# Block 1's rope, global and dilated attention in one section with a written order of PE, DVE and ACT

## The chip, the cores and the metric

The kernel runs on one core of one Trainium2 chip. The metric is the device time of one execution in microseconds. Five engines work side by side, each on its own list of instructions in order: TensorE (PE, matmuls and transposes), VectorE (DVE), ScalarE (ACT), GpSimd (POOL) and SyncE (SP, which issues most transfers).

## The reference

A network of two layers is run on 256 tokens of width 1024: first Block 1 of both layers, then Block 2 of both. The change touches the mixer of Block 1 only:

```python
proj = h @ w_in
qa, ka, va, qd, kd, vd, gates = split(proj)             # 512, 128, 128, 768, 768, 768, 2048
qa = apply_rope(rms_norm(qa, qn_g)); ka = apply_rope(rms_norm(ka, kn_g))
out_a = global_gqa(qa, ka, va)                          # 8 heads of 64, 2 k/v heads, softmax over 256 keys
out_b = dilated(qd, kd, vd)                             # 12 heads in 3 groups, distance bias, softmax over all 3 groups
g_a, g_b = split(sigmoid(gates))
merged = g_a * (out_a @ w_pa) + g_b * (out_b @ w_pb)
return merged @ w_o
```

Behind it stand a residual with layer norms, and a mixture of 16 experts with a router. Six vectors per layer (shifts, scales and gates) come from a matrix `ada` times the conditioning vector.

## The kernel before, in words

All weights are float32 and are streamed once. A block of 1 MB lands in one of four raw buffers (`wraw`, issued by SP in program order). ACT casts each half of it to a rounded float (`hi`, L60, tile `whi`), DVE subtracts to get the rest (`lo`, L66, tile `wlo`), and PE does three matmuls in place of one: data-high by weight-high, data-low by weight-high, data-high by weight-low (`mm3`, L251 to L253). A block of w_in is 48 such matmuls of 256 columns (blocks 9 and 10, the dilated v, 24 of 512).

Each `ada` piece is four more 1 MB blocks, summed on DVE: two scalar-times-matrix sums of 128x1024 a block (L465, L467), then a few tiny matmuls with ones (`ada_cols`, `ada_row`). The loads are spread as background work: `wblk` pops one (`tick`) after each weight block, and the attention parts pop some by the tables `TJ` and `TU`. The sums of a load come at the next tick (`settle`).

Block 1's mixer (L951) starts when q, k and v of the global attention stand in PSUM. 17 weight jobs remain: three blocks of dilated q, three of k, three of v (one PSUM bank each for two token halves in the first two), eight of gates. Between them: rope and RMS norm of q and k on DVE (the norm factor is multiplied into q, L1017, and k, L1021), transposes of q and k on PE (L1028, L1033) with copies on ACT; then four pairs of global heads: scores (L1044), maximum on DVE, exponential on ACT (L379), shares on DVE (L385), transposes on PE (L392), copies on ACT (L395), values (L404). Then four dilated steps (two head pairs by two token halves): scores (L1092), bias on DVE (L1097), exponentials, shares, transposes (L1116), copies (L1118), values. The jobs are closures in a list, and `fill` puts one between two attention parts. Within this program order a scheduler chooses the order of instructions on each engine from its own estimates, so a cast can move ahead of a copy that was written before it. PSUM has two banks for scores and small sums (`sb`), two for transposes (`tp`) and four for products (`acc`).

Behind the mixer come w_pa (2 blocks), w_pb (1), w_out (4), the router's weights and the experts (16).

Of the kernel before, what the change touches and what calls it, by code (L numbers as in the profile page):

```python
# [15 lines left out]
DEPTH = 2  # L16
# [156 lines left out]
class Net:  # L173
    def __init__(self, tc, a, out, ctx, dbg=None):
        self.tc, self.nc, self.a, self.out = tc, tc.nc, a, out
        self.dbg_hook = dbg
        self.ctx = ctx
        P = lambda name, bufs, **k: ctx.enter_context(tc.tile_pool(name=name, bufs=bufs, **k))
        self.const = P("const", 1)
        self.big = P("big", NB8)  # L180
        self.wr = P("wr", NRAW)
        self.wh = P("wh", NHL)
        self.wl = P("wl", NHL)
        self.bg = []
        self.fills = []
        self.pend = None
# [256 lines left out]
    def ada_piece(self, l, pc, fin, row=False):  # L443
# [15 lines left out]
        def add(k, r):  # L459
            acc = box["acc"]  # L460
            for i in range(2):
                f = 2 * k + i
                rv = r[:, i * D:(i + 1) * D]
                if f == 0 and not row:
                    nc.vector.tensor_scalar_mul(acc, rv, self.cond[:, 0:1])  # L465
                else:
                    nc.vector.scalar_tensor_tensor(acc, rv, self.cond[:, f:f + 1], acc, op0=OP.mult, op1=OP.add)  # L467
            if k == 3:
                fin(acc)

        def go(k):
            r = load(k)
            self.settle()
            self.pend = lambda: add(k, r)
        return [lambda k=k: go(k) for k in range(4)]

    def settle(self):

        if self.pend:
            self.pend()  # L480
            self.pend = None

    def ada_cols(self, l, acc, dst, f0, n, off, j, plus):

        nc = self.nc
        ps = self.sb()
# [7 lines left out]
    def ada_row(self, acc, scale):  # L494
# [3 lines left out]
        for h in range(2):  # L498
            ps = self.tp()
# [451 lines left out]
    def mixer(self, l, hT):  # L951
# [17 lines left out]
        gt = [self.b8([128, 8, 256], name="gate") for _ in range(2)]  # L969

        def fm_job(i, dst, func, scale, ps=None):
            hl = self.wblk(w[i], 8)
            ps = self.fm_bank(hT, hl, 0, 8, ps=ps and ps())
            nc.scalar.activation(dst, ps, func, scale=scale)

        def vd_job(dst, n, srcs):
            bk, = self.proj_tm(hT, [(srcs, n)])
            for t in range(2):
                nc.scalar.copy(dst[:, t], bk[t])
        for dst, i0, sc in ((qdT, 3, 0.125), (kdT, 6, 1.0)):  # L980
            for b in range(3):
                self.fills.append(lambda i=i0 + b, d=dst[:, 2 * b:2 * b + 2], sc=sc:
                                  fm_job(i, d, AF.Copy, sc, self.sb if i < 3 + NSB[l] else None))
        self.fills.append(lambda: vd_job(vd0, 512, [w[9], w[10]]))
        self.fills.append(lambda: vd_job(vd1, 256, [w[11]]))
# [4 lines left out]
        qrs = []  # L990
        krs = []
        for t in range(2):
            nc.scalar.copy(va[:, t], kva[t][:, 128:256])
            for which, src, nh in ((0, qa[t][:, :512], 8), (1, kva[t][:, :128], 2)):
                rs = self.head_rstd(src, nh)
                if which == 0:
                    v = self.small([128, 16], "rs8", 2)
                    nc.vector.tensor_scalar_mul(v[:, :nh], rs, 0.125)
                    rs = v[:, :nh]
                A = self.t2([128, nh, 64], name="ropeA")  # L1000
                B = self.t2([128, nh, 32, 2], name="ropeB")
                s3 = src.rearrange("p (h d) -> p h d", d=64)
                s4 = src.rearrange("p (h d e) -> p h d e", d=32, e=2)
                cc = rt[:, which, t, 0][:, None, :].to_broadcast([128, nh, 64])
                nc.vector.tensor_mul(A, s3, cc)
                sv = rt[:, which, t, 1].rearrange("p (d e) -> p d e", e=2)
                for e in range(2):
                    nc.vector.tensor_mul(B[:, :, :, e], s4[:, :, :, 1 - e],
                                         sv[:, None, :, e].to_broadcast([128, nh, 32]))
                nc.vector.tensor_add(A, A, B.rearrange("p h d e -> p h (d e)"))  # L1010
                o = self.t2([128, 512], name="roped")
                rb = rs[:, :, None].to_broadcast([128, nh, 64])
                if which == 0:

                    for s in range(2):
                        ov = o.rearrange("p (j s d) -> p j s d", j=4, s=2)[:, :, s]
                        nc.vector.tensor_mul(ov, A[:, s * 4:(s + 1) * 4],  # L1017
                                             rs[:, s * 4:(s + 1) * 4, None].to_broadcast([128, 4, 64]))
                    qrs.append(o)
                else:  # L1020
                    nc.vector.tensor_mul(o[:, :128].rearrange("p (h d) -> p h d", d=64), A, rb)  # L1021
                    krs.append(o)
        for jj in range(2):
# [7 lines left out]
        p = self.tp()  # L1031
        for t in range(2):
            nc.tensor.transpose(p[:, t * 128:(t + 1) * 128], krs[t][:, :128], self.ident)  # L1033
        nc.scalar.copy(kaT, p[:, :256])
        oa = self.b8([128, 2, 4, 256], R, name="oa")
        zz = self.small([128, 2, 8], "att_z", 2)

        def scores(j):
            pr = []
            for h in range(2):  # L1040
                s = self.sb()
                hs = slice(h * 64, (h + 1) * 64)
                for t in range(2):
                    nc.tensor.matmul(s[:, t * 256:(t + 1) * 256], qaT[hs, j, t * 128:(t + 1) * 128], kaT[hs, :],  # L1044
                                     start=True, stop=True)
                n = 2 * j + h
                pr.append(self.exps(s.rearrange("p (n w) -> p n w", n=2), [zz[:, t, n:n + 1] for t in range(2)]))
            return pr

        def values(j, pr):  # L1050
            rz = self.small([128, 2, 2], "att_rz", 2)
            nc.vector.reciprocal(rz, zz[:, :, 2 * j:2 * j + 2])
            pts = []
            for h in range(2):
                self.share(pr[h], rz[:, :, h])
                pts.append(self.p_fm(pr[h]))
            if j % 2 == 0:
                bank["o"] = self.acc("oacc")
            o = bank["o"][:, j % 2 * 256:(j % 2 + 1) * 256]
            self.two_heads(o, [[pt[:, c] for c in range(2)] for pt in pts],  # L1060
                           [[va[:, c, h * 64:(h + 1) * 64] for c in range(2)] for h in range(2)])
            self.split_to(oa[:, 0, j], oa[:, 1, j], o)
        bank = {}
        self.bg_on = True
        for j in range(4):
            pr = scores(j)
            if j == 1:
                nc.gpsimd.dma_start(d01, a["k_dist"][:, :, 0:2])
                nc.gpsimd.dma_start(d2, a["k_dist"][:, :, 2])
            if j in TJ[l]:  # L1070
                self.tick()
            self.fill()
            values(j, pr)
        if l == DEPTH - 1:
            self.decay_log(0)

        self.fill(len(self.fills))
        for i in range(2):
            for b in range(4):
                self.fills.append(lambda i=i, b=b: fm_job(12 + 4 * i + b, gt[i][:, 2 * b:2 * b + 2], AF.Tanh, 0.5))  # L1080
        ob = self.sm.tile([128, 2, 2, 256], R, name="ob", tag="s4b", bufs=2)
        zz = self.small([128, 2, 8], "att_z", 2)
        od = self.acc("obacc")
        for jp in range(2):
            for t in range(2):
                sb = [self.sm.tile([128, 3, 256], F, name="sbias", tag="z1", bufs=NZ1) for _ in range(2)]
                for gs in ((0, 1), (2,)):
                    ss = [self.sb() for _ in range(2)]
                    for g in gs:
                        for i in range(2):  # L1090
                            hs = slice(i * 64, (i + 1) * 64)
                            nc.tensor.matmul(ss[i][:, g % 2 * 256:(g % 2 + 1) * 256],  # L1092
                                             qdT[hs, 2 * g + jp, t * 128:(t + 1) * 128], kdT[hs, 2 * g + jp, :],
                                             start=True, stop=True)
                    for g in gs:
                        for i in range(2):
                            nc.vector.scalar_tensor_tensor(sb[i][:, g], dist[t][g], -SLOPES[4 * g + 2 * jp + i],  # L1097
                                                           ss[i][:, g % 2 * 256:(g % 2 + 1) * 256],
                                                           op0=OP.mult, op1=OP.add)
                rz = self.small([128, 2], "att_rz", 2)  # L1100
                pts = []
# [844 lines left out]
```

## Time and profile before

| | us |
|---|---|
| median of 3 runs (lowest, highest) | 1745.29 (1740.69, 1746.53) |
| the profiled execution | 1744.94 |
| its span, first to last instruction | 1743.1 |
| Block 1's section, layer 0 (56.30 to 236.60) | 180.3 |
| Block 1's section, layer 1 (492.40 to 668.50) | 176.1 |

The section is counted from the end of the qkv matmuls to the first matmul of w_out. The mean granted clock of PE over the span is 0.984 of full speed. In the tables of stretches the columns are the stretch, its length, then busy microseconds of each engine with the number of instructions in brackets, the granted clock of PE, the share of the DMA engines and GB/s.

### The profile page before, as it was taken

Reading aid. Unit: us, or ns where it says so; the run is one execution under the profiler, and the core shown is the slowest. Engines: PE = TensorE matmul, PEld = TensorE weight load, DVE = VectorE, ACT = ScalarE, POOL = GpSimd, SP = SyncE. Lnnn points to the kernel's source line nnn. Section 1 sums busy time; section 2 is a strip of 40 time slices with the busy share of each in tenths; the row PEclk is TensorE's granted clock in tenths of the full one; section 3 lists DMA queues with packets and bytes.
Section 4 is the critical chain, followed back from the end, with each engine's and each line's share of the span. In section 5 each row is a group of like instructions: output and inputs, shape, how many; then the busy total and the mean of one; then the engine's idle time right before and its main releaser. Section 6 shows DMA issues by size and latency. Waiting matters only on the chain. (4 is left out here: it accounts for less than half of the span.)

```text
span 1743.1 us, 26009 instructions
## 1 busy us (share of the span) xinstructions
PE 1667.9 (96%) x10498; PEld 1451.3 (83%) x10498; DVE 1219.7 (70%) x1657; ACT 890.6 (51%) x1272; POOL 155.0 (9%) x187
## 2 busy tenths in 40 slices
PE   7899998999989999899999999999999999999999
PEld 6788886777778898677778889899987888989997
DVE  7888788879888857887986575655546457565453
ACT  1555446667554445666755454444435345454442
POOL 2200022200120002110020300000001120000000
PEclk9899999999999999989999999999999999999999
DMA  8777662889677744388965534455555463545551
GB/s 317 289 272 274 236 250 89 317 311 341 224 251 265 274 161 140 122 318 316 352 240 196 175 134 170 172 181 192 173 194 218 139 216 121 171 152 187 186 180 70
DMA packets 56334, 374.09 MB, mean 215 GB/s; under 512 B 6896, under 2 KB 7056, under 8 KB 14224
## 3 DMA queue, kind: packets, MB, share of 16 engines
q1 hardware_dynamic: 50256, 352.41, 56.4%
q0 software_dynamic: 5952, 19.97, 3.5%
q8 instruction: 84, 1.38, 0.3%
q14 instruction: 42, 0.34, 0.1%
HBM read 370.25 MB, written 2.10 MB: 214 GB/s over the span
## 5 line engine op out<-in xcount | busy, mean ns | idle before, releaser
L66 DVE TENSOR_TENSOR wlo<-wraw,whi 128x1024 fp32r<-128x1024 f32 x562 | 675.6, 1222 | 308.2 <-ACT whi L60 303.7
L60 ACT CAST whi<-wraw 128x1024 fp32r<-128x1024 f32 x572 | 587.6, 1049 | 437.3 <-PE acc L252 207.2
L251 PE MATMUL acc<-fm_hi,whi 128*128 128x256 f32 x1536 | 440.0, 286 | 0.0
L252 PE MATMUL acc<-fm_lo,whi 128*128 128x256 f32 x1536 | 436.0, 284 | 0.0
L253 PE MATMUL acc<-fm_hi,wlo 128*128 128x256 f32 x1536 | 435.5, 284 | 0.0
L251 PEld LDWEIGHTS acc<-fm_hi,whi 128*128 128x128 f32 x1536 | 294.7, 192 | 10.0 <-issue 8.9
L252 PEld LDWEIGHTS acc<-fm_lo,whi 128*128 128x128 f32 x1536 | 295.1, 192 | 3.7 <-issue 3.7
L253 PEld LDWEIGHTS acc<-fm_hi,wlo 128*128 128x128 f32 x1536 | 294.9, 192 | 1.8 <-issue 1.8
L262 POOL TENSOR_TENSOR rs_r<-rs_v,mhalf 128x1 f32<-128x1 f32 (+3 forms) x52 | 58.6, 1128 | 973.0 <-DVE rs_v L261 965.8
L251 PE MATMUL acc<-whi,fm_hi 128*128 128x512 f32 (+1 forms) x384 | 137.6, 360 | 3.1 <-ACT fm_hi L323 3.1
L253 PE MATMUL acc<-whi,fm_lo 128*128 128x512 f32 (+1 forms) x384 | 135.7, 354 | 4.2 <-DVE fm_lo L324 4.1
L252 PE MATMUL acc<-wlo,fm_hi 128*128 128x512 f32 (+1 forms) x384 | 135.9, 354 | 1.3 <-DVE wlo L66 1.3
L251 PE MATMUL gu<-whi,hgh 128*128 128x512 f32 x256 | 106.2, 415 | 5.1 <-DVE dT L669 2.9
L252 PE MATMUL gu<-wlo,hgh 128*128 128x512 f32 x256 | 103.7, 405 | 1.5 <-DVE wlo L66 1.5
L253 PE MATMUL gu<-whi,hgl 128*128 128x512 f32 x256 | 102.7, 401 | 0.0
L467 DVE SCALAR_TENSOR_TENSOR ada_acc<-wraw,cond,ada_acc 128x1024 f32<-128x1024 f32 x74 | 94.5, 1277 | 0.8
L253 PEld LDWEIGHTS acc<-whi,fm_lo 128*128 128x128 f32 x384 | 74.5, 194 | 15.1 <-DVE fm_lo L324 5.7
L252 PEld LDWEIGHTS acc<-wlo,fm_hi 128*128 128x128 f32 x384 | 74.5, 194 | 13.6 <-DVE wlo L66 4.9
L251 PEld LDWEIGHTS acc<-whi,fm_hi 128*128 128x128 f32 x384 | 74.4, 195 | 13.3 <-ACT fm_hi L323 4.1
L251 PE MATMUL acc<-whi,act_hi 128*128 128x512 f32 x176 | 68.5, 389 | 0.0
L252 PE MATMUL acc<-wlo,act_hi 128*128 128x512 f32 x176 | 68.5, 389 | 0.0
L253 PE MATMUL acc<-whi,act_lo 128*128 128x512 f32 x176 | 68.5, 389 | 0.0
(386 smaller groups left out, 2612.1 us busy)
## 6 DMA issues: line engine op xcount, KB each, us to landing
wraw<-in_moe SPq DMA_DIRECT2D x96, 1024.0 KB, 5.4
wraw<-in_win SPq DMA_DIRECT2D x58, 1024.0 KB, 5.4
wraw<-in_ffi SPq DMA_DIRECT2D x44, 1024.0 KB, 4.8
wraw<-in_ada SPq DMA_DIRECT2D x40, 1024.0 KB, 5.0
wraw<-in_wg SPq DMA_DIRECT2D x32, 1024.0 KB, 4.9
wraw<-in_ffo SPq DMA_DIRECT2D x22, 1024.0 KB, 4.8
wraw<-in_wo SPq DMA_DIRECT2D x16, 1024.0 KB, 4.9
wraw<-in_ada SPq DMA_DIRECT2D x16, 512.0 KB, 7.9
```

The costliest lines, as they stand in the source:

```text
L60: net.nc.scalar.copy(h, self.r[:, i * 1024:(i + 1) * 1024])
L66: (eng or net.nc.vector).tensor_sub(l, self.r[:, i * 1024:(i + 1) * 1024], h.bitcast(F))
L251: mm(ps, l[0], r[0], start=first, stop=False)
L252: mm(ps, l[0], r[1], start=False, stop=False)
L253: mm(ps, l[1], r[0], start=False, stop=last)
L262: nc.gpsimd.tensor_tensor(r[:, :n], v[:, :n], self.mhalf[:, :n], op=OP.pow)
L467: nc.vector.scalar_tensor_tensor(acc, rv, self.cond[:, f:f + 1], acc, op0=OP.mult, op1=OP.add)
```

## The change

The rope, the global attention, the dilated attention and the 17 weight jobs become one section in which the order of PE, DVE and ACT is the order in which the code is written. POOL and SP are still placed by the scheduler. The section is built from small pieces (`hi`, `lo`, `mm`, `ev`, `S`, `X`, `N`, `T`, `V` and, for the dilated part, `DS`, `DX`, `DN`, `DT`, `DV`). Block n+1 is cast and split while block n is multiplied, in step n. From step 3 on, each step loads one `ada` block and does the two sums of the one before at two places (`t0`, `t1`); before, 24 blocks were loaded in layer 0's section, now 14, and the other ten go behind it. Their last tiny matmuls are put off to the next tick and use an `acc` bank. The q norm factor is no longer multiplied into q: it scales the scores inside the exponential (a second per-partition operand) and the maximum (a tiny DVE multiply). Shares of the second head of each pair and all dilated shares move from DVE to ACT, and copies of transposed shares go back into the same tile.

```diff
-        self.fill(2)                                   # first two jobs, rope and attention between fills
-        for j in range(4):
-            pr = scores(j)
...
-            if j in TJ[l]:
-                self.tick()
-            self.fill()
-            values(j, pr)
...
+        def X(j):
...
+                nc.vector.tensor_reduce(nm[:, :2], s3, axis=AX.X, op=OP.max, negate=True)
+                nc.vector.tensor_tensor(nm[:, :2], nm[:, :2], rsq[:, :, n], op=OP.mult)
+                p = self.t2([128, 2, 256], name="prob")
+                for t in range(2):
+                    nc.scalar.activation(p[:, t], s3[:, t], AF.Exp, bias=nm[:, t:t + 1], scale=rsq[:, t, n:n + 1],
+                                         accum_out=zz[:, t, n:n + 1])
...
+        self.defer = True
+        with self.tc.manual_schedule(engines={E.DVE, E.Activation, E.PE}):
...
+            for i in range(4):
+                mm(0, i)
+            ev(0)
+            load(2)
+            rope(0, 0)
+            hi(1, 0)
+            lo(1, 0)
+            for t in range(2):
+                k_norm(t)
+            rope(1, 0)
+            k_tr()
+            hi(1, 1)
+            lo(1, 1)
...
+            for i in range(2):
+                mm(1, i)
+            q_tr(0)
+            mm(1, 2)
+            q_tr(1)
+            mm(1, 3)
+            ev(1)
+            load(3)
+            hi(2, 0)
+            lo(2, 0)
+            hi(2, 1)
+            lo(2, 1)
+            S(0)
+            X(0)
+            for i in range(4):
+                mm(2, i)
+            ev(2)
+            hi(3, 0)
+            lo(3, 0)
+            N(0)
+            hi(3, 1)
+            lo(3, 1)
...
+            for j in range(4):
+                n = 3 + j
+                load(n + 1)
+                t0, t1 = self.tick2()
+                if j < 3:
+                    S(j + 1)
+                    hi(n + 1, 0)
+                    X(j + 1)
+                else:
+                    DS(0, (0, 1))
+                    hi(n + 1, 0)
+                T(j)
+                mm(n, 0)
+                lo(n + 1, 0)
+                do(t0)
+                hi(n + 1, 1)
+                V(j)
+                mm(n, 1)
...
+                lo(n + 1, 1)
+                do(t1)
+                for i in (2, 3):
+                    mm(n, i)
+                ev(n)
+            if l == DEPTH - 1:
+                self.decay_log(0)
...
+            for u in range(4):
+                n = 9 + 2 * u
+                load(n + 1)
+                t0, t1 = self.tick2()
+                if u < 3:
+                    DS(u + 1, (0, 1))
+                hi(n + 1, 0)
+                DT(u)
+                lo(n + 1, 0)
+                do(t0)
+                mm(n, 0)
+                mm(n, 1)
+                hi(n + 1, 1)
+                if u < 3:
+                    DS(u + 1, (2,))
+                DV(u)
+                lo(n + 1, 1)
...
+                ev(n)
+                n += 1
+                load(n + 1)
+                t0, t1 = self.tick2()
+                hi(n + 1, 0)
+                lo(n + 1, 0)
+                mm(n, 0)
+                mm(n, 1)
...
+                ev(n)
+            self.sums()
```

In the order of ACT at the opening of the section in layer 0, `dil<-sb` is the eviction of a dilated q job, `sq` a square for a norm, `kaT` the copy of the transposed k. Before:

```order
15 L60 CAST whi<-wraw 128x1024 x2
16 L279 ACTIVATE sq<-acc 128x512
17 L60 CAST whi<-wraw 128x1024 x2
18 L279 ACTIVATE sq<-acc 128x128
19 L974 ACTIVATE dil<-sb 128x512
20 L279 ACTIVATE sq<-acc 128x512
21 L60 CAST whi<-wraw 128x1024 x2
```

and after:

```order
11 L60 CAST whi<-wraw 128x1024 x4
12 L1210 COPY va<-acc 128x128 x2
13 L281 ACTIVATE sq<-acc 128x128 x2
14 L1026 ACTIVATE dil<-sb 128x512
15 L60 CAST whi<-wraw 128x1024
16 L1087 COPY kaT<-tp 128x256
17 L60 CAST whi<-wraw 128x1024
```

The casts of the second job's block stood ahead of the first eviction; now the two halves of that block stand behind it, with the k copy between them.

DVE at the same place (`wlo` is a remainder of a weight block, `ropeA` and `roped` parts of rope, L1072 the k norm). After:

```order
40 L1055 TENSOR_TENSOR ropeA<-acc,ropeg 128x512
41 L1058 TENSOR_TENSOR ropeB<-acc,ropeg 128x256 x2
42 L1067 TENSOR_TENSOR roped<-ropeA,ropeB 128x2x4x64
43 L66 TENSOR_TENSOR wlo<-wraw,whi 128x1024
44 L1072 TENSOR_TENSOR ropeA<-ropeA,rs_r 128x128 x2
45 L1055 TENSOR_TENSOR ropeA<-acc,ropeg 128x512
```

The k norm, which the first transposes need, stands behind the remainder of the second block.

DVE at the router of layer 0 (`lg` logits, `sel` the choice, `s` and `gs` its sums by groups). Before:

```order
233 L66 TENSOR_TENSOR wlo<-wraw,whi 128x1024
234 L1180 TENSOR_TENSOR lg<-sb,br 128x32
235 L1189 TENSOR_TENSOR sel<-sg,rbias 128x32
236 L1196 TENSOR_TENSOR s_2746<-sel 128x8x3
237 L1196 TENSOR_TENSOR s_2746<-sel 128x8x2
```

and after:

```order
227 L66 TENSOR_TENSOR wlo<-wraw,whi 128x1024
228 L1405 TENSOR_TENSOR lg<-sb,br 128x32
229 L467 SCALAR_TENSOR_TENSOR ada_acc<-wraw,cond,ada_acc 128x1024
230 L1414 TENSOR_TENSOR sel<-sg,rbias 128x32
231 L467 SCALAR_TENSOR_TENSOR ada_acc<-wraw,cond,ada_acc 128x1024
232 L1421 TENSOR_TENSOR s_2702<-sel 128x8x3
```

Two sums of an `ada` block stand in the chain now.

## Rows read from the trace of the kernel before

**Rows 1.** The page's busy table: busy time, share of the span, instructions

```profile
PE 1667.9 (96%) x10498; PEld 1451.3 (83%) x10498; DVE 1219.7 (70%) x1657; ACT 890.6 (51%) x1272; POOL 155.0 (9%) x187
```

**Rows 2.** Table by stretches: the section's two parts, layer 1's section, two places behind

```profile
56.30:98.30 42.00, 35.33 (x243) 30.61 (x241) 35.80 (x66) 18.10 (x38) 6.32 (x6) 0.88 0.69 256
98.30:236.60 138.30, 136.32 (x1034) 119.28 (x1032) 111.97 (x148) 66.84 (x115) 6.08 (x8) 1.00 0.74 272
...
492.40:668.50 176.10, 167.03 (x1256) 147.69 (x1255) 133.28 (x215) 85.60 (x153) 18.79 (x26) 0.98 0.67 240
...
230.00:240.00 10.00, 8.52 (x55) 7.17 (x55) 9.17 (x14) 6.01 (x10) 1.36 (x2) 1.00 0.68 254
...
330.00:340.00 10.00, 10.00 (x48) 8.12 (x46) 9.46 (x11) 7.93 (x10) 0.00 (x0) 1.00 0.97 374
```

**Rows 3.** PE's waits in layer 0's section: total us, times, longest

```profile
PE sb L1044 <- ACT prob L379: 3.6, 1, 3.6
...
PE acc L251 <- DVE mr L1135: 0.2, 1, 0.2
```

**Rows 4.** PE's waits in layer 1's section

```profile
PE oacc L404 <- ACT pt L395: 2.6, 1, 2.6
PE acc L251 <- DVE mr L1135: 1.8, 1, 1.8
...
PE sb L1092 <- DVE sbias L1097: 0.2, 1, 0.2
```

**Rows 5.** PE in order of time (start, length), and one line's sum

```profile
62.42 0.28 PE L251 MATMUL sb<-fm_hi,whi 128*128 128x256 f32 x1
62.54 0.28 PE L252 MATMUL sb<-fm_lo,whi 128*128 128x256 f32 x1
...
98.42 0.70 PE L1044 MATMUL sb<-kaT,qaT 64*128 64x256 f32 x2
...
139.94 1.14 PE L1092 MATMUL sb<-dil 64*128 64x256 f32 x8
...
L1092 PE MATMUL sb<-dil 64*128 64x256 f32 x48 | 10.6, 424 | 0.4 <-DVE sbias L1097 0.3
```

**Rows 6.** ACT by line and shape, 56 to 240: busy us, mean ns

```profile
L60 ACT CAST whi<-wraw 128x1024 fp32r<-128x1024 f32 x42 | 42.7, 1049 | 13.0 <-PE acc L252 7.2 <-DMA wraw<-in_win 3.3 <-PE acc L253 2.5
...
L379 ACT ACTIVATE prob<-sb,sm_nm 128x256 f32<-128x256 f32 x16 | 7.4, 474 | 1.2 <-DVE sm_nm L376 1.2
...
L1118 ACT COPY ptd<-tp 128x256 f32<-128x256 f32 x8 | 3.1, 383 | 0.0
...
L974 ACT ACTIVATE dil<-sb 128x512 f32<-128x512 f32 x2 | 1.2, 597 | 7.3 <-PE sb L253 7.3
```

**Rows 7.** DVE by line and shape, layer 0 (last row layer 1)

```profile
L467 DVE SCALAR_TENSOR_TENSOR ada_acc<-wraw,cond,ada_acc 128x1024 f32<-128x1024 f32 x44 | 56.2, 1278 | 0.5
L66 DVE TENSOR_TENSOR wlo<-wraw,whi 128x1024 fp32r<-128x1024 f32 x38 | 45.9, 1217 | 5.7 <-ACT whi L60 5.5
...
L376 DVE TENSOR_REDUCE sm_nm<-sb 128x2 f32<-128x512 f32 x8 | 5.3, 683 | 0.8 <-PE sb L1044 0.8
...
L385 DVE TENSOR_SCALAR prob<-prob,att_rz 128x256 f32<-128x256 f32 x16 | 4.5, 346 | 0.0
...
L1021 DVE TENSOR_TENSOR roped<-ropeA,rs_r 128x128 f32<-128x128 f32 x2 | 0.6, 282 | 0.0
...
L1506 DVE TENSOR_SCALAR dec_p<-dec_p 128x8 f32<-128x8 f32 x8 | 1.3, 163 | 0.1
```

**Rows 8.** The page's DMA issues: KB each, median us to landing

```profile
wraw<-in_win SPq DMA_DIRECT2D x58, 1024.0 KB, 5.4
...
wraw<-in_ada SPq DMA_DIRECT2D x16, 512.0 KB, 7.9
```

**Rows 9.** DVE in order of time at the router, layer 0

```profile
282.70 0.18 DVE L1180 TENSOR_TENSOR lg<-sb,br 128x32 f32<-128x32 f32 x1
283.18 0.19 DVE L1189 TENSOR_TENSOR sel<-sg,rbias 128x32 f32<-128x32 f32 x1 [0.29 <-ACT sg L1183]
```

More of the change, by code (lines that the diff above doesn't have):

```diff
@@ L969, in mixer @@
         gt = [self.b8([128, 8, 256], name="gate") for _ in range(2)]
[L971 to L983, printed above, removed]
@@ L984, in mixer, with load, bank @@
-        self.fills.append(lambda: vd_job(vd0, 512, [w[9], w[10]]))
-        self.fills.append(lambda: vd_job(vd1, 256, [w[11]]))
-        self.fill(2)
-        va = self.small([128, 2, 128], "va", 1)
+        va = self.small([128, 2, 128], "va", 1)
+        oa = self.b8([128, 2, 4, 256], R, name="oa")
+        box = {}
+        def load(n):
+            if n < 17:
+                blk[n] = Block(self, w[3 + n], 4 if n in (6, 7) else 8)
+        def bank(n):
+            if n not in banks:
+                banks[n] = self.sb() if n < 2 else self.acc()
+            return banks[n]
@@ L988, in mixer, with hi, lo, do @@
+        blk, banks = {}, {}
+        def hi(n, i):
+            if n < 17:
+                blk[n].hi(i)
+        def lo(n, i):
+            if n < 17:
+                blk[n].lo(i)
+        def do(pieces):
+            for f in pieces:
+                f()
         qaT = self.sm.tile([128, 4, 256], F, name="qaT", tag="grow", bufs=2)
         kaT = self.sm.tile([128, 256], F, name="kaT", tag="kaT", bufs=1)
[L990 to L1010, printed above, removed]
-                o = self.t2([128, 512], name="roped")
[L1012 to L1022, printed above, removed]
@@ new lines, in mixer, with DS @@
+        zd = self.small([128, 2, 8], "att_z", 2)
+        def DS(u, gs):
+            jp, t = u // 2, u % 2
+            if gs[0] == 0:
+                box["d", u] = [self.sm.tile([128, 3, 256], F, name="sbias", tag="z1", bufs=NZ1) for _ in range(2)]
+            sb = box["d", u]
+            ss = [self.sb() for _ in range(2)]
+            for g in gs:
+                for i in range(2):
+                    hs = slice(i * 64, (i + 1) * 64)
+                    nc.tensor.matmul(ss[i][:, g % 2 * 256:(g % 2 + 1) * 256],
+                                     qdT[hs, 2 * g + jp, t * 128:(t + 1) * 128], kdT[hs, 2 * g + jp, :],
+                                     start=True, stop=True)
+            for g in gs:
+                for i in range(2):
+                    nc.vector.scalar_tensor_tensor(sb[i][:, g], dist[t][g], -SLOPES[4 * g + 2 * jp + i],
+                                                   ss[i][:, g % 2 * 256:(g % 2 + 1) * 256], op0=OP.mult, op1=OP.add)
@@ new lines, in DX, with DN @@
+        def DX(u, i):
+            sv = box["d", u][i].rearrange("p g w -> p (g w)")[:, None, :]
+            z = zd[:, u % 2, 2 * (u // 2) + i:2 * (u // 2) + i + 1]
+            self.exps(sv, [z], 1, 768, True)
+        def DN(u):
+            c = 2 * (u // 2)
+            rz = self.small([128, 2], "att_rzd", 2)
+            nc.vector.reciprocal(rz, zd[:, u % 2, c:c + 2])
+            for i in range(2):
+                sv = box["d", u][i].rearrange("p g w -> p (g w)")
+                nc.scalar.activation(sv, sv, AF.Copy, scale=rz[:, i:i + 1])
```

304 lines of the change are left out of this document (205 added, 99 removed).

## The prediction

> **What bounds the kernel now.** I read the busy table first [rows 1]: TensorE (PE) is busy for 96% of the span, VectorE (DVE) for 70%, ScalarE (ACT) for 51%. The end is therefore set by PE's work plus the few places where PE stands still, and an operation taken from DVE or ACT is worth only what it takes out of a PE wait. The table by stretches [rows 2] then says where the changed part lies: Block 1's section from the end of the qkv matmuls to the first matmul of w_out takes 42.0 + 138.3 = 180.3 us in layer 0 and 176.1 us in layer 1. The first 42 us run at a mean clock of 0.88, so part of them at the lower of the two levels (1.2 GHz, 0.5). The list of PE's waits in each section comes third [rows 3, 4]. It gives seven waits of 3.6 (for ACT's exponentials) down to 0.2 us in layer 0, together 7.2, and in layer 1 seven of 2.6 to 0.2, together 9.0, of which 0.2 and 1.8 lie at the gates that the change leaves alone. Nearly everything after 98 us runs without a wait. So there are three things to win per layer: the waits, what the clock lost after them, and score matmuls that stand alone instead of in pairs.
>
> **What goes.** Durations are from the profiled execution (1744.94 us, span 1743.1), 0.35 us under the median of 1745.29, so a difference against one is a difference against the other.
> Waits: 7.0 us in layer 0, 7.2 in layer 1. Clock: in layer 0, 42 x 0.12 = 5.0 us of work were lost to it; in layer 1, 176.1 x 0.02 = 3.5, half of it behind the gates' wait, which stays: 1.7. Pairs: eight score records in one go take 1.14 us, a pair alone 0.70 [rows 5], so four records about 0.8. After the change a layer has 4 x (1.14 + 0.8) = 7.8 us of dilated scores where the row has 10.6: 2.8 go. The global scores of two of the four heads stop being split, and each lone pair then costs a quarter of the eight, 0.29 instead of 0.70: 0.8. Together 3.6 us a layer. The q multiplies that go into the exponential were on DVE's path to the q transposes and lie in the waits already counted. Sum: -(7.0 + 5.0 + 3.6) = -15.6 us in layer 0, -(7.2 + 1.7 + 3.6) = -12.5 in layer 1.
>
> **What is new: PE, DVE and ACT in strict order.** The written order puts each block's cast and remainder right behind the eviction of the block before, and small steps behind the casts. Each engine takes its rows in turn, so I walked the three lists with the durations of [rows 6, 7].
> (a) The k transposes now follow block 0 directly. ACT first evicts (0.60), casts half of block 1 (1.05), DVE takes the remainder (1.22) and then normalizes k (2 x 0.28): 3.4 us from the end of block 0, with PE idle. Before, block 1 was already split and PE ran on.
> (b) The second quarter of block 1 waits for the copy of k (0.38), a cast and a remainder, 2.6 us, beside 12 matmuls of 0.12 us [rows 5]: 1.2 us. (c) The first scores want both score banks, and one is held by block 1's result until its eviction: 0.5. (d) Block 2 waits for eviction, cast and remainder, 2.9 us, less (c) and the scores: 1.2. (e) The first transposes of the shares wait for eviction, cast, remainder, reciprocal and two shares, 3.7 us, beside the next scores: 2.3. (f) The first values wait until ACT has done two shares (moved there from DVE), two casts, four exponentials and two copies: 8.6 us after block 2's end by the rows, when PE, with (e), has work for 5.7: 2.9. (A copy of 512 is taken at the 0.60 of the eviction of that shape, a reciprocal at the 0.16 of the tiny operations.) Together 11.5 us.
> (g) For the next two heads ACT has eviction, cast, exponentials (which start when scores and a maximum of 0.68 are through, about 2 us) and copies before the values, 4.9 us; PE has scores, transposes and 12 matmuls, 3.5 us: 1.4 each, 2.8.
> (h) The dilated transposes fill two banks, and the third group waits for an ACT copy that now stands behind an eviction and a cast: 0.65 us three times and 1.6 at the last, where no scores stand before: 3.6 if the cast's weights are there. They may not be: per step one weight block and one ada block are loaded now, a block of this matrix takes 5.4 us to land, in the slowest group of such loads 7.9 [rows 8], and every second step offers PE only 48 x 0.12 = 5.76 us. 5.4 makes nothing late; 7.9 makes it 3.6 + 4 x 2.1 = 12. I take 6, nearer to the row of the matrix itself.
> (i) The w_pa block is split only after the section ends: 1.5, between 0 and a cast and remainder in series (2.3). (j) Clock: the longest new wait is near the 3.6 us of layer 0, behind which 5.0 us were lost, and the 2.6 us of layer 1, behind which 1.7 were. I take 1.7, bounds 0 and 5.0.
> The exponentials get a second per-partition operand. No row shows one with two; with one, an ACTIVATE of 256 takes 474 ns against 383 for a plain copy [rows 6], so 0 to 0.09 us each. The Trainium skill (ScalarE: Activation LUTs, What ACT_TABLE_LOAD costs) gives about 93 ns for each such pointer operand. The trace agrees for the first operand, 91 ns by the two rows. By that rule the four exponentials of a head grow by 0.37 us and stand whole in (f) and (g), 1.1 us a layer; at nothing, the sum stays. That sum is 11.5 + 2.8 + 6 + 1.5 + 1.7 = 23.5 in either layer, and I leave the operand at nothing.
>
> Layer 1 has two more. Its first block is split in the section, so the second half of block 0 waits for a remainder: 1.2. The logarithm of the decay, 22 tiny DVE operations of 0.16 us that come some 0.2 us apart [rows 7], stood spread between other work; now they stand as one run of 4.4 us ahead of block 8's remainders, and block 8 starts some 2.7 us late (between 0 and 4.4).
>
> **Sum of the sections.** Layer 0: 23.5 - 15.6 = +7.9. Layer 1: 27.4 - 12.5 = +14.9. Counted the other way, PE's own work after is 114.6 us for 20 blocks (18 of 5.76, two of 5.45), about 42 for all scores, transposes, values and ada sums, and the waits: 157 + 23.5 = 180.5 in layer 0 (+0), 184.4 in layer 1 (+8). The two counts differ by switches between operand kinds that I can't price from rows; I take the middle, +4 and +11.
>
> **Behind layer 0's section.** Before, its section took 24 ada blocks (44 of the 48 sums in one row of [rows 7]); now it takes 14, and the other ten go into w_pa, w_pb, w_out (7) and the experts (3). Their 20 sums of 1.28 us fall where DVE is as good as full: 9.17 of 10 us at 230 to 240 [rows 2]. Two of them stand between the router's logits, its choice and its sums of groups, a chain that PE waits on, with 0.3 us of slack [rows 9]: 2 x 1.19 - 0.3 = 2.1. Two stand before the remainders of the expert inputs: about 1.5. The three experts' loads come where DMA is at 0.97 and 374 GB/s [rows 2]; a block more is at most 2.5 us each, but DVE and PE set the pace there, so 0.4 of 7.5. Taken: +4 (0 to +11).
>
> Sum: 4 + 11 + 4 = +19, **1764 us**.
>
> **Rivals.**
> Faster. ACT and DVE run ahead: if casts are through before the eviction that I put ahead of them ends up mattering, (f), (g) and (h) vanish, since only work already queued separates them. For it: ACT is busy only 66.84 of 138.30 us [rows 2], so there is room for a lead. Against it: the rows are in strict order, and each cast stands behind an eviction that needs PE's last matmul. Price: (f) to (h), 11.7 us a layer, is gone and 3.6 of clock and decay with it: 19 - 27 = -8, about 1737. It decides as soon as V's copies end inside 12 matmuls.
> No change. The waits come as in the lower count (0 and +8) and the tail costs nothing beyond it because the ten blocks hide as they did before: with (h) at 3.6 and (i) at 0 it is 8 - 4.8 - 3 = 0, 1745. For it: the lower count has no unpriced part. Against: two sums do stand in the chain of [rows 9], where nothing else fills PE.
> Later still. Transfers set the steps: (h) at 12 in both layers, the experts' loads at +7.5 instead of 0.4: 19 + 12 + 7 = 38, about 1783; a clock that falls in these waits only fills them. For it: DMA is 0.74 busy in this section already and ada and weights now alternate strictly. Against: the ten blocks that leave make 10 MB less here. The Trainium skill (TensorE: Matmul & The Clock Gate, A second HAM failure mode) warns that frequent short idles of PE between groups make the clock go up and down. No row of this kernel shows that for idles under 1 us: after 98.30 the clock is 1.00 [rows 2] with waits of 0.2 to 0.3.
>
> **How the numbers follow.** Slower as forecast 0.47, later still 0.12, faster 0.26, no change 0.15. A measurement of this kernel tells 0.3% (5 us) from nothing; of the forecast's own spread (1752 to 1775) nearly all is above 1750, so slower is 0.60, same 0.14, faster 0.26. The range leaves out the fastest and the latest tenth: 1735 to 1779.
>
> **What would show it.** A PE wait of some 3 us before the k transposes and again before the first values; PE clock below 1 between 56 and 98; no DVE wait for q rope; scores of a head as one group; ACT copies behind casts at the dilated transposes; in layer 1 DVE's decay run ahead of a PE wait; in layer 0 DVE sums between the router's rows. The forecast is wrong if the section of layer 0 falls below 172 us, if the w_out starts of both layers come earlier than 236.6 and 668.5 in their stages, or if weights land late in the dilated part so that DMA and not ACT ends the waits.

## The result and the profile after

The changed kernel takes 1820.88 us (median of 4 runs, 1816.0 to 1823.09) against 1745.83 us: 1.0433 times the time before, 95% interval 1.0402 to 1.0464. I had forecast 1764 us and a range that ended at 1779. The direction was right, the size was not: +75 us where I had +19.

The busy table of the changed kernel's page (to be read against [rows 1]): PE is busy 25 us longer in a span that is 78 us longer, with the same 10498 instructions.

```profile
PE 1692.6 (93%) x10498; PEld 1476.2 (81%) x10498; DVE 1210.4 (66%) x1621; ACT 912.2 (50%) x1302; POOL 156.1 (9%) x187
```

The same number of instructions takes longer, and the granted clock in the next table is lower than before; the rest of the longer span is waiting. The table by stretches of the changed kernel shows layer 0's section, the stretch up to layer 1's section, and layer 1's section (columns as in [rows 2]; the third last is PE's granted clock):

```profile
59.07:256.96 197.89, 173.61 (x1260) 153.97 (x1258) 126.01 (x171) 98.11 (x167) 18.52 (x23) 0.93 0.57 207
256.96:531.21 274.25, 248.45 (x1118) 197.77 (x1117) 227.86 (x303) 160.10 (x215) 29.24 (x32) 0.94 0.70 256
531.21:740.05 208.84, 176.05 (x1256) 157.24 (x1255) 131.86 (x208) 100.10 (x172) 20.04 (x27) 0.90 0.53 192
```

Against before these are 197.9 for 180.3, 274.3 for 255.8 (from 236.63 to 492.39, clock 0.97 there) and 208.8 for 176.1: +17.6, +18.5 and +32.7. Before the first section lie 2.8 us more and behind the last 6.7, where PE has the same matmuls. Over all the profiles of this case the stretch ahead takes 56.0 to 59.1 us and the one behind 1068.7 to 1081.5, with the same matmuls each time, so these 9.5 us are no more than profiles differ by there.

PE's waits in layer 0's section of the changed kernel, in place of [rows 3] (total, times, longest):

```profile
PE acc L503 <- DVE ada_acc L467: 6.1, 2, 4.2
PE oacc L406 <- ACT prob L1130: 5.0, 3, 2.3
PE tp L1179 <- ACT sbias L1181: 3.9, 4, 3.0
PE tp L1086 <- DVE ropeA L1072: 3.1, 1, 3.1
PE acc L515 <- DVE ada_acc L467: 3.0, 1, 3.0
PE tp L1128 <- DVE prob L387: 2.3, 1, 2.3
PE acc L255 <- DVE wlo L66: 0.6, 1, 0.6
```

and in layer 1's, in place of [rows 4]:

```profile
PE acc L503 <- DVE ada_acc L467: 11.0, 2, 9.1
PE oacc L406 <- ACT prob L1130: 6.6, 3, 3.8
PE tp L1179 <- ACT sbias L1181: 5.4, 4, 4.5
PE tp L1086 <- DVE ropeA L1072: 3.1, 1, 3.1
```

L503 and L515 are the column and row sums that end an ada piece; L406 the values, L1179 the dilated transposes, L1086 the k transposes, L1128 the transposes of the shares. The lists add up to 24.0 and 32.7 us (before 7.2 and 9.0). The clock's share, by the windows, is 197.89 x 0.07 = 13.9 and 208.84 x 0.10 = 20.9 us, where before it was 5.0 and 3.5; in layer 1 some 3 us of that fall into waits. So layer 0 grew by 16.8 of waits and 8.5 to 9 of clock and gave back 7 to 8 in PE's own work; layer 1 grew by 23.7 of waits and 14 to 17 of clock and gave back about 8.

The longest wait, in layer 1, seen on DVE, ACT and PE of the changed kernel (start, length, in brackets the idle time before and its releaser):

```profile
617.62 0.17 DVE L1734 SCALAR_TENSOR_TENSOR dec_l<-dec_x,dec_p 128x8 f32<-128x8 f32 x1
617.70 0.16 DVE L1167 RECIPROCAL att_rzd<-att_z 128x2 f32<-128x2 f32 x1
...
620.68 1.23 DVE L66 TENSOR_TENSOR wlo<-wraw,whi 128x1024 fp32r<-128x1024 f32 x1 [2.76 <-ACT whi L60]
621.82 1.28 DVE L467 SCALAR_TENSOR_TENSOR ada_acc<-wraw,cond,ada_acc 128x1024 f32<-128x1024 f32 x1
623.02 1.22 DVE L66 TENSOR_TENSOR wlo<-wraw,whi 128x1024 fp32r<-128x1024 f32 x1
624.15 1.28 DVE L467 SCALAR_TENSOR_TENSOR ada_acc<-wraw,cond,ada_acc 128x1024 f32<-128x1024 f32 x1
```

```profile
617.96 1.76 ACT L1170 ACTIVATE sbias<-sbias,att_rzd 128x768 f32<-128x768 f32 x2 [4.70 <-DVE dec_p L1728]
619.62 1.98 ACT L60 CAST whi<-wraw 128x1024 fp32r<-128x1024 f32 x2
```

```profile
625.58 0.56 PE L503 MATMUL acc<-ones,ada_acc 128*128 128x1 f32 x2 [9.09 <-DVE ada_acc L467]
```

PE ended block 7 at 616.5 and could not begin its column sums before 625.6. The decay run holds a reciprocal back, the reciprocal ACT's two shares, the shares the casts of block 8, the casts DVE's remainders, and the column sums want DVE's last sum of that step, which stands behind all of them. Every link is short; the written order makes one chain of them.

### The profile page after: what moved, and what is told of

Read it like the earlier page. It is cut to its first block, busy times and chain, and to the rows that moved or that the text cites. A ratio compares the mean times of both kernels' runs of the same rounds, so it can differ in the third digit from the quotient of the medians.

```text
span 1821.3 us, 25976 instructions
## 1 busy us (share of the span) xinstructions
PE 1692.6 (93%) x10498; PEld 1476.2 (81%) x10498; DVE 1210.4 (66%) x1621; ACT 912.2 (50%) x1302; POOL 156.1 (9%) x187
## 5 line engine op out<-in xcount | busy, mean ns | idle before, releaser
L253 PE MATMUL acc<-fm_hi,whi 128*128 128x256 f32 x1536 | 447.2, 291 | 0.0
L255 PE MATMUL acc<-fm_hi,wlo 128*128 128x256 f32 x1536 | 440.4, 287 | 1.3 <-DVE wlo L66 1.3
L254 PE MATMUL acc<-fm_lo,whi 128*128 128x256 f32 x1536 | 440.7, 287 | 0.0
L253 PEld LDWEIGHTS acc<-fm_hi,whi 128*128 128x128 f32 x1536 | 301.3, 196 | 9.3 <-issue 8.0
L255 PEld LDWEIGHTS acc<-fm_hi,wlo 128*128 128x128 f32 x1536 | 300.7, 196 | 2.4 <-DVE wlo L66 1.7
L254 PEld LDWEIGHTS acc<-fm_lo,whi 128*128 128x128 f32 x1536 | 301.0, 196 | 1.6 <-issue 1.5
L264 POOL TENSOR_TENSOR rs_r<-rs_v,mhalf 128x1 f32<-128x1 f32 (+3 forms) x48 | 50.7, 1059 | 992.9 <-DVE rs_v L263 985.7
```

The lines of the kernel that those rows point to most:

```text
L253: mm(ps, l[0], r[0], start=first, stop=False)
L254: mm(ps, l[0], r[1], start=False, stop=False)
L255: mm(ps, l[1], r[0], start=False, stop=last)
L264: nc.gpsimd.tensor_tensor(r[:, :n], v[:, :n], self.mhalf[:, :n], op=OP.pow)
```

## Experiments

Two theories stood against each other: that the strict order of the three engines makes the loss, through waits and the clock, or that the pieces and the fewer ada blocks in the section do.

**x_sched: the order given back.**

```diff
-        with self.tc.manual_schedule(engines={E.DVE, E.Activation, E.PE}):
+        with ExitStack():
```

> The changed kernel with the written order of PE, DVE and ACT given back to the scheduler in Block 1's section; the pieces, the moved shares, the norm in the exponential and the 14 ada blocks in the section stay. Theory A (the strict order makes the waits, each wait lowers PE's clock): waits and half-speed stretches of the two sections (56.7 us of waits, 68 us at half speed in the changed kernel) fall back to about the 17 us and 17 us of the kernel before, and what stays is the ada overflow behind layer 0's section: about 1821 - 50 - 10 = 1755 to 1765 us. Rival B (the pieces themselves and the fewer ada blocks make the loss, whoever orders them): 1800 us or more.

1726.14 us (1722.22 to 1728.27), 0.9902 of the kernel before (0.9882 to 0.9922): faster than before, and 95 us faster than the written order of the same pieces. Its stretches:

```profile
57.55:217.45 159.90, 158.74 (x1260) 143.16 (x1258) 133.11 (x177) 96.58 (x166) 20.23 (x23) 1.00 0.77 281
217.45:483.35 265.90, 246.22 (x1115) 195.45 (x1116) 223.64 (x301) 161.54 (x216) 29.65 (x32) 0.96 0.69 252
483.35:647.70 164.35, 158.22 (x1256) 143.70 (x1255) 130.31 (x208) 97.32 (x170) 20.48 (x27) 0.98 0.73 255
```

Layer 0's section runs at full clock with one wait of 0.3 us. Layer 1's has one long wait left:

```profile
PE tp L1128 <- DVE prob L387: 5.8, 1, 5.8
```

DVE's reciprocal and shares stand there behind the first operation of the decay, for which DVE idled 6.5 us until a load had landed: an order that the scheduler chose can hold a late row, too. Theory A was right on the cause and too small on the effect; rival B falls. The pieces are worth 20.4 and 11.8 us in the sections against the kernel before.

**x_only_act, x_only_dve, x_only_pe, x_act_dve: which engine's order.** The set in the same line is cut to one engine, or to ACT and DVE.

> The changed kernel with the written order kept for ACT alone; DVE and PE are ordered by the scheduler. All three written gave 1821 us, none written 1726. Theory G (ACT's order, each cast behind an eviction that needs PE's last matmul, is the main loss): 1790 us or more. Rival H (DVE's order, sums and remainders ahead of what PE waits for): under 1760.

> The changed kernel with the written order kept for DVE alone. Theory G (ACT's order is the main loss): 1730 to 1760 us. Rival H (DVE's order): 1790 or more.

> The changed kernel with the written order kept for PE alone. Theories G and H agree: PE's own order only groups the matmuls, 1725 to 1735 us. Rival I (PE's order puts column sums and transposes where nothing else can be slipped in front, so the order of the other two would do no harm by itself): 1780 or more here, and under 1760 in the other two.

> The changed kernel with the written order kept for ACT and DVE together; PE is ordered by the scheduler. One engine alone written cost +3.5 (PE), +12 (ACT) and +35 (DVE) over 1726 us, together 51, where all three cost 95. Theory J (ACT and DVE lock each other: cast and remainder of one block wait for each other in one fixed place, whatever PE does): 1800 us or more. Rival K (the locks need PE's order too: matmuls that PE can't slip in front of column sums and transposes): 1765 to 1785, about the sum of the two.

| written | median us | over 1726.1 | ratio to before (interval) |
|---|---|---|---|
| PE | 1729.6 | 3.5 | 0.9915 (0.9889 to 0.994) |
| ACT | 1737.94 | 11.8 | 0.9961 (0.9946 to 0.9977) |
| DVE | 1761.44 | 35.3 | 1.0112 (1.0075 to 1.0149) |
| ACT and DVE | 1780.34 | 54.2 | 1.0196 (1.0179 to 1.0214) |
| all three | 1820.88 | 94.7 | 1.0433 (1.0402 to 1.0464) |

Theory G falls, and so does rival I (1729.6 where it had 1780 or more): ACT's order alone still leaves a kernel slightly faster than before. H has the right engine, at half its size. J falls and K holds: PE's order costs 3.5 us alone, which is within what runs of one kernel differ by here (1722 to 1728, 1726 to 1731), and 40.5 on top of the other two. My reading, which no run shows by itself: while one engine is free it slips its work past the other's late row; with all three written, nothing does. Of DVE's 35 us by the profiles about a third each lies in the two sections (171.6 for 159.9, 177.2 for 164.4) and in the stretch between them (276.6 for 265.9).

**x_dve_late: the ada sums' places.** With only DVE written, both sums of a step move from within it to its end:

```diff
-                do(t0)
...
-                do(t1)
...
                 ev(n)
+                do(t0 + t1)
```

> Only DVE's order written (1761 us), with the two ada sums of a step at its end, behind all that the step's own chain asks of DVE, instead of at two places within it. Theory P (DVE's written order costs 35 us because sums of 1.28 us whose block has landed late stand ahead of remainders and maxima): 1735 to 1748. Rival Q (it costs them by the order of the small operations and remainders itself, which stand behind ACT's casts): 1755 or more.

1770.92 us (1768.4 to 1773.05), 9.5 us slower than DVE written with the sums inside. Theory P's forecast falls. The run doesn't show Q's reading by itself, though: in layer 0 PE's waits at the dilated transposes fell from 3.7 to 2.2 us, and those at the column and row sums, which want the later `ada` sums, grew from 4.3 to 7.2. So one cost was changed for another, and which rows make DVE's 35 us stays open.

**x_sums: column sums later, decay behind the section.**

```diff
         def go(k):
-            self.sums()
+            if not self.defer:
+                self.sums()
...
                 mm(n, 1)
+                self.sums()
...
-            if l == DEPTH - 1:
-                self.decay_log(0)
             DN(0)
```

> The changed kernel, order of all three engines still written, with two edits: the column sums of an ada piece come after the second quarter of a step's matmuls instead of at its start, and the decay's 22 operations come behind the section. In the changed profile PE waits 4.2 and 1.9 us (layer 0), 9.1 and 1.9 us (layer 1) at these sums. Theory N (they hold PE up themselves: the sum they need is DVE's last of the step before): those waits shrink to the remainder that the block itself needs, 10 to 12 us of waits and 3 to 7 us of clock go, 1803 to 1809. Rival O (the block behind would wait as long for its own remainder, so the sums only show the wait first): 1815 or more.

1796.77 us (1793.37 to 1797.88), 24 us less than 1820.88. N holds, beyond its size, but for two edits at once. In layer 0, where no decay stands, the section gets 6.2 us shorter (191.7), in layer 1, where both edits act, 19.0 (189.8); the run doesn't part the two there. In layer 0 the waits at the sums have gone; what is left (first rows):

```profile
PE oacc L406 <- ACT prob L1131: 5.5, 3, 2.8
PE tp L1180 <- ACT sbias L1182: 5.3, 4, 2.8
PE tp L1087 <- DVE ropeA L1073: 3.1, 1, 3.1
PE acc L255 <- DVE wlo L66: 2.9, 4, 1.4
```

**x_ahead: everything cast one step earlier, still written.** Loads come two steps earlier too, and so ahead of the ada block's.

```diff
-                load(n + 1)
+                load(n + 3)
...
-                hi(n + 1, 0)
+                hi(n + 2, 0)
...
-            ev(0)
-            load(2)
-            rope(0, 0)
-            hi(1, 0)
-            lo(1, 0)
+            hi(2, 0)
+            ev(0)
+            load(3)
+            rope(0, 0)
```

> The changed kernel with the order of all three engines still written, but each block cast and split one step earlier (block n+2 in step n), in the opening ahead of the evictions, and loaded two steps before. Theory L (the loss is the chain eviction, cast, remainder between PE's end of one block and the next thing PE needs; a written order is harmless once that chain has a step of slack): the waits at the opening, the values, the column sums and the dilated transposes shrink from 56.7 us to under 25 in the two sections, 1750 to 1775 us. Rival M (a written order loses it elsewhere, since the order of small operations is not what their times ask for): 1795 or more.

1793.07 us (1790.91 to 1799.08): 28 us gained, between the two theories. Its sections take 186.3 and 195.0 us. The wait for the k transposes has gone, but the values' wait has grown from 5.0 to 8.2 us in layer 0, because the casts now stand in front of the exponentials instead; the column sums wait as before:

```profile
PE oacc L406 <- ACT prob L1130: 8.2, 3, 5.4
PE acc L503 <- DVE ada_acc L467: 6.1, 2, 4.2
```

A step of slack mends the chain that I had walked and moves the wait to the next one. M's point, that the order of small operations isn't what their times ask for, stays.

**x_wfirst: weights loaded ahead of ada blocks.**

```diff
+            load(4)
             for j in range(4):
                 n = 3 + j
-                load(n + 1)
+                load(n + 2)
```

> The changed kernel with each weight block's load issued ahead of the ada block's of its step instead of right behind it. In the changed profile the two are issued 1.2 us apart, the first lands after 4.9 us and the second after 7.1 to 7.7. Theory F (late weights hold the casts back and these the copies, shares and remainders behind them on ACT and DVE): PE's waits at the column sums and at the dilated transposes shrink, 8 to 15 us faster, 1806 to 1813. Rival (the waits come from the order of the evictions and casts alone): within 3 us of 1821.

1810.23 us (1808.66 to 1816.01), 11 us less: in the range of theory F, for half of its reason. The waits at the dilated transposes fell from 3.9 and 5.4 to 2.1 us in either layer, but layer 0's waits at the column sums are the same 6.1 us in its profile; late weights are a small part.

**x_fill and x_fill2: the clock by itself.** Small matmuls on ones go into PE's waits, nothing else changes. x_fill2 halves the numbers of x_fill.

```diff
+        def warm(n, ps):
+            for _ in range(n):
+                nc.tensor.matmul(ps[:, :256], self.ones, self.ones[:, None, :].to_broadcast([128, 2, 128]),
+                                 start=True, stop=True)
+        FILL = dict(a=(6, 6), e=(4, 4), f=(4, 7), g=(2, 2), s8=(8, 19), s12=(3, 3), t=(6, 9), end=(6, 2))
...
+            fill("a", self.sb)
             k_tr()
```

> The changed kernel with small matmuls on ones (128x256, not part of the computation, 0.21 us each at full speed) put on PE into its longest known waits of Block 1's sections, each group shorter than the wait it stands in. No wait is taken away. Theory A (half of the loss is PE's clock, which falls after each wait): half-speed time in the two sections falls from 68 us to under 20, and the kernel gets about 20 to 25 us faster, near 1797. Rival C (the clock only falls where PE waits anyway, so the waits alone are the loss): no faster, or 2 to 6 us slower for the added matmuls and the switches between kinds of operands, 1821 to 1827.

1821.46 us (1817.03 to 1828.71): no gain at a mean clock of 0.982, by its number in the range of rival C. But the groups had the wrong size, which was my error: 172 records of 0.216 us instead of 86 in layer 0. They overran the waits (the sections took 205.0 and 212.1 us for 197.9 and 208.8, at a clock of 0.98 and 1.00), so the run tells nothing between A and C.

> As the earlier kernel with small matmuls on ones in PE's longest waits, but with half as many: each had run as two matmuls of 0.216 us, so the groups had been twice as long as the waits (33.5 and 54 us of them against 24 and 33 us of waits) and the clock's gain was eaten. Theory A (the clock falls after waits and costs 13 and 17 us in the two sections): now the groups fit, the sections run at full speed and the kernel gets 15 to 25 us faster than 1821, 1796 to 1806. Rival C (clock lost only where PE waits anyway): 1817 to 1825.

1802.59 us (1799.43 to 1809.3), 18 us faster by added work. The sections:

```profile
56.33:251.94 195.61, 184.35 (x1341) 161.23 (x1340) 127.02 (x172) 98.56 (x168) 17.60 (x23) 0.97 0.59 217
...
524.00:719.72 195.72, 185.89 (x1365) 163.11 (x1363) 132.58 (x209) 100.06 (x173) 19.93 (x27) 0.99 0.57 208
```

The clock rises from 0.93 and 0.90 to 0.97 and 0.99, which by the windows is worth 8 and 19 us; layer 1's section is 13 us shorter, layer 0's only 2. There the added matmuls (19.3 us busy) and the waits that were left (10.9) came to 30.2 us in place of the 24.0 us of waits. Theory A holds, the sections at 0.97 and 0.99 and not quite at full speed: the clock is a loss of its own. Of the 18 us some 15 lie in the two sections, about a sixth of the 95 us.

**x_noada: without the ten ada blocks behind layer 0's section** (their vectors stay at zero or half summed).

> The changed kernel without the loads and sums of the ten ada blocks of layer 0 that the change pushed behind its section (their vectors are left at zero or half summed). Theory D (their DVE sums and their transfers cost the 18.7 us that the stretch between the two sections grew by): that stretch falls from 274 us to about 256 and the kernel to about 1803. Rival E (the stretch grew by clock and by order, not by this work): 1815 or more. My prediction's own term was 4 us: 1817.

1796.52 us (1794.26 to 1800.86), 24 us less. By the kernel's time theory D is exceeded, but not by the stretch that it named, which falls by 12.7 us and not by 18.7:

```profile
256.78:518.30 261.52, 246.99 (x1115) 196.66 (x1116) 206.92 (x288) 159.72 (x213) 30.00 (x33) 0.95 0.64 232
```

The rest of the gain lies in layer 1's section (204.0 us for 208.8) and behind it (1073.9 for 1081.3, no more than profiles differ by there); none of the ten blocks stands in either. So the ten blocks are worth 12.7 us where they stand; the cause of the rest stays open.

**x_sched24: the scheduler's order and all 24 ada blocks in layer 0's section again.**

```diff
+        def extra():
+            if self.bg:
+                self.bg.pop(0)()
...
             ev(0)
             load(2)
+            extra()
```

and so after blocks 1 and 2, heads 1 to 3 and the four dilated steps.

> The changed kernel with all three engines ordered by the scheduler (1726 us), and in layer 0's section 24 ada blocks again instead of 14, so that none is left for w_pa, w_out and the experts. In the 1726 us run the stretch behind layer 0's section has 19.5 us of PE waits, among them 4.6 at the branch of the experts and 2.1 at the router, against 13.9 in the kernel before. Theory D (the ten blocks cost what they delay there): 10 to 16 us faster, 1710 to 1716. Rival (their sums slow the section instead by as much, or the scheduler had hidden them): 1722 to 1730.

1708.42 us (1707.11 to 1709.66), 0.9798 of the kernel before (0.9775 to 0.982): 17.7 us less than x_sched and the fastest of all, better than both kernels. Theory D holds and is exceeded.

```profile
55.98:216.54 160.56, 159.55 (x1275) 144.87 (x1274) 144.27 (x190) 96.88 (x167) 17.99 (x23) 1.00 0.86 314
216.54:471.74 255.20, 244.18 (x1103) 195.35 (x1102) 210.18 (x289) 161.68 (x216) 27.13 (x32) 0.95 0.66 241
471.74:630.98 159.24, 157.10 (x1256) 142.75 (x1255) 126.27 (x207) 97.50 (x170) 20.47 (x27) 1.00 0.74 262
```

DVE is busy 11 us longer in layer 0's section than in x_sched (144.27 for 133.11), and the section is as long, 160.6 for 159.9: the sums are all but free there. The stretch behind is 10.7 us shorter, and layer 1's section 5.1 us, where the wait of 5.8 us is gone.

**x_norm: the norm in the exponential alone, on the kernel before.** Its edits are those of `X` and of the q branch of `rope` in the change.

> The kernel before with one part of the change alone: the q norm factor goes into the exponential's scale and the maximum, and the multiplies of q go. My prediction put its gain inside PE's waits for the q transposes (2 times 1.4 us) and the second operand at 0 to 0.09 us each. If that holds: 0 to 6 us faster, 1738 to 1744. Rival (the longer exponentials and the two tiny multiplies stand on the chain to the shares): 1744 to 1748.

1740.47 us, ratio 0.9975 (0.9963 to 0.9987): 4 us faster. The first wait of [rows 3] falls from 3.6 to 2.6 us.

## Why the prediction was wrong, step by step

What bounds the kernel was read rightly: PE's work, its waits, the clock behind them. What goes (15.6 and 12.5 us) was about right: in x_sched waits and clock went wholly in layer 0 (in layer 1 the one wait of 5.8 us and a clock of 0.98 are left), and PE's own work fell by 7 to 8 us where the pairs had 3.6.

The waits that I walked came as walked: (a) 3.1 for 3.4, (e) 2.3 for 2.3, (f) 2.3 and 3.8 for 2.9, (g) 1.4 each for 1.4. (h) came near its 6 with 3.9 and 5.4 by luck: the three first waits were 0.3 for 0.65 each, the last 3.0 and 4.5 for 1.6, and the 7.9 us that I had taken for the slowest loads is the row of half as large ones. (b) to (d) came to 0.6 us in layer 0 and 1.2 in layer 1 for 2.9, the second half of layer 1's block 0 to 1.1 for 1.2. (i), 1.5 for w_pa, showed no wait of its own. I missed the column and row sums: 9.1 us in layer 0, 12.6 in layer 1, of which 2.7 stood in the sum as the late block 8. The code calls `self.sums()` at a step's start; I had read it as work put off, and not asked which DVE row it waits for. x_sums shows what that costs.

The step that failed most is (j), the clock: 1.7 us a layer, bound 5.0, so 1.7 us of loss after the change in layer 0 and, with what stays behind the gates' wait, about 3.5 in layer 1, where the windows give 13.9 and 20.9. I had priced one wait of 3 us, as the trace of before had it. There were nine of 1.4 to 4.2 us in layer 0 and ten of 1.1 to 9.1 in layer 1. In slices of 4 us of the profile the clock falls in seven places in layer 0 and in five in layer 1, each of them behind one or two waits of 1.9 us or more. Three such slices of layer 0, the first two around a wait of 1.4 us for the values, the third behind the wait of 4.2:

```profile
104.00:108.00 4.00, 2.63 (x21) 2.43 (x22) 3.42 (x6) 3.50 (x11) 0.00 (x0) 1.00 0.20 80
108.00:112.00 4.00, 4.00 (x30) 3.17 (x30) 2.15 (x5) 2.47 (x5) 0.00 (x0) 1.00 0.00 0
144.00:148.00 4.00, 3.87 (x18) 3.90 (x19) 0.28 (x2) 1.55 (x2) 0.25 (x1) 0.50 0.87 342
```

In x_only_act, where no wait of the sections is over 1.5 us, both run at 1.00. I had quoted the Trainium skill's warning (TensorE: Matmul & The Clock Gate, A second HAM failure mode) and set it aside because waits of 0.2 to 0.3 us left the clock alone; the trace of the change agrees with it as far as the clock goes down and up, with 0.90 on average in layer 1. x_fill2 shows what the clock alone gives back: 18 us, some 15 of them in the two sections.

Second, the place behind layer 0's section: +4 forecast, +18.5 measured. The two sums at the router were right (PE waits 2.1 us for `mem`, where it waited 0.2 before). I missed the loads. The first two waits of the stretch:

```profile
PE acc L254 <- DVE wlo L66: 6.5, 3, 5.0
PE acc L1539 <- DVEq L1571: 4.6, 1, 4.6
```

The 5.0 us in the first are a block of w_mkv whose remainder is late: its cast waited 3.50 us for a load that now stands behind ada blocks, and the remainder then stood behind y's chain on DVE. It takes both parts of the change: the wait is gone in x_noada, which has the written order without the ten blocks, and in x_sched, which has the ten blocks without the written order; with DVE's order alone (x_only_dve) it is there. The stretch is 10.1 us longer than before in x_sched and 8.4 more in the changed kernel; x_noada takes 12.7 off it, and 24 off the kernel.

Third, where my two counts differed I took the middle without a reason that a row gave. The higher one (+7.9 and +14.9) was nearer to +17.6 and +32.7. And the rivals were wrong in kind: I asked whether the waits would be hidden, never whether the same pieces, in the scheduler's order, would be the faster kernel.

The exponential's second operand came out at 561 ns for the 474 of [rows 6]:

```profile
L1110 ACT ACTIVATE prob<-sb,sm_nm,rsq 128x256 f32<-128x256 f32 x16 | 8.8, 561 | 2.2 <-DVE sm_nm L1107 1.7 <-PE tp L1128 0.5
```

87 ns, so the Trainium skill's 93 ns for such an operand (ScalarE: Activation LUTs, What ACT_TABLE_LOAD costs) was the better of the two ends; it is small beside the rest.

What stays open: x_only_dve and x_dve_late say that DVE's order costs, and that later places for the ada sums don't mend it, but no run singles out which rows do it; nor does any run show why PE's order costs 40.5 us on top of the other two.

## What to carry to other kernels

A written order on several engines at once is only as good as every link in it: before writing one, take the same pieces with the scheduler's order as the measure, and write one engine at a time; here no written order beat it. When a sum of waits is made for PE, price the clock behind every long wait, not once. And ask of every step that is put off which row it then stands behind, on each queue, the load queue included.

## What the runs showed of the hardware

The wait of 4.6 us is put down to DVE's queue at the experts' branch (`DVEq L1571`), but it isn't the branch: DVE's two operations before it had become long, in the changed kernel's rows,

```profile
383.02 3.44 DVE L66 TENSOR_TENSOR wlo<-wraw,whi 128x1024 fp32r<-128x1024 f32 x1
386.38 2.82 DVE L412 TENSOR_TENSOR yy<-yg,yy 128x512 fp32r<-128x512 f32 x1
```

where the same operations take 1.22 and 0.68, while POOL ran the like:

```profile
382.99 5.66 POOL L66 TENSOR_TENSOR wlo<-wraw,whi 128x1024 fp32r<-128x1024 f32 x2 [40.90 <-ACT whi L60]
```

Before, POOL's two remainders of that place took 4.73 us from 345.44 on, and no DVE operation grew beside them: those that ran there (`si`, `yg`, `at`, 0.48, 0.69 and 0.42 us) each read a PSUM tile. At another place of the kernel before one did grow, the second of two like operations, the first of which ended as POOL began:

```profile
467.33 0.55 DVE L166 TENSOR_SCALAR z<-x,ln_nmu,rs_r 128x512 f32<-128x512 f32 x1 [0.44 <-POOL rs_r L262]
467.79 2.38 POOL L66 TENSOR_TENSOR wlo<-wraw,whi 128x1024 fp32r<-128x1024 f32 x1
467.80 2.65 DVE L166 TENSOR_SCALAR z<-x,ln_nmu,rs_r 128x512 f32<-128x512 f32 x1
```

The Trainium skill (GPSIMD Engine Reference, Specifications) says that GpSimd shares its ways into SBUF with VectorE and contends with operations that have two SBUF inputs; the trace agrees, with 3.44 for 1.22; it shows the same for `z`, which has one large input. A delay of some microseconds in another stage was enough to bring the two together; in x_noada, without the ten blocks, they stand apart again and the 4.6 us are gone.
